# Staging the split output weights in the recurrent branch instead of the gating branch

## The chip, the cores and the metric

The kernel runs on one core of a Trainium2 chip. TensorE (PE) does the matmuls, VectorE (DVE), ScalarE (ACT) and GpSimd (POOL) the elementwise work, SyncE (SP) issues most loads. The time is that of one execution on the device in microseconds (us); less is better.

## What is computed

Two layers (DEPTH = 2) over 1024 tokens of width 1024. Each layer norms x, projects it through one input matrix `w_in`, runs three branches (a recurrent one, latent attention, and causal spatial gating, "SGU"), norms and gates the branches, and projects them through `w_out`:

```python
def spatial_gating(u, v, norm_g, norm_b, w_s, b_s):
    u = jax.nn.gelu(u)
    v = layer_norm(jax.nn.gelu(v), norm_g, norm_b)
    ...
# each layer:
#   x <- x + RMSNorm_post( W_out( concat_g RMSNorm_g( branch_g * SiLU(gate_g) ) ) )
# recurrent branch: h[t] = a[t] * h[t-1] + b[t], with a, b from gates of a short convolution of x
```

## The kernel before

All is float32, and every matmul is done in three passes over operands split in a high part and a remainder, hi x hi, hi x lo and lo x hi (`mm3`, L124 to L126). So each weight block must be split before it is used: ACT copies the high part, and POOL or DVE subtracts it to get the low part. For weights of `w_in` this is class `W` (loads at L366, ACT copy L375, subtract L376, on DVE for the columns `C_U` and `C_GC`, on POOL otherwise), for all else `split` (ACT copy L356, subtract L357).

A layer goes through these stages: the normed x is turned to feature rows hT; the recurrent branch runs in `group(g, half)`, six feature blocks in two halves of the tokens (convolution `conv`, gates `gate_in`, and for each of three blocks a chain of `lru_steps` that ends in a scan, L493, and L498); its steps wait in a list `pend` and are handed out a few at a time by `drain`. Then the SGU branch: a loop over eight token tiles with 512 columns (`toks` with the weights `C_U`, gelus L676 and L679, statistics L677 and L678), the turn of `sgu_w` (L691), the rope tables in layer 0 (among them L265, and L307), a loop over eight tiles with 256 columns (tanh L706 on ACT, then L707 on DVE, weights `wgc`), `sgu_mix` (L663) and a loop with the 352 columns of the latents (`C_LAT`). Attention and the output projection follow.

Large buffers come from a pool `FS` of seven slots F0 to F6 (rows of the result tile Y are lent to it), a first-in first-out list: a load into a slot waits until the last reader of the slot's former content is done. The register names R and H are smaller pools. A scheduler orders the instructions of each engine by a simulated timeline, so an engine's order is not the text's; each engine then runs its own order strictly.

Eight blocks of 128 rows of `w_out` (`wo0` to `wo7`) are split early in each layer and kept in DRAM, high parts `wo_h` and low parts `wo_l`, from where they are read in attention. `stage_wo(n)`, called once in each of the 16 steps of the two SGU loops, does it: in an even step it takes two slots and loads a block (SP, 512 KB, L615), in the odd step behind it ACT scales the block if it is one of the last three (L619) and copies the high part (L356), POOL subtracts (L357), ACT's queue stores the high part (L621), POOL's queue the low part (L622), and both slots are given back.

Of the kernel before, what the change touches and what calls it, by code (L numbers as in the profile page):

```python
# [8 lines left out]
F32R = mybir.dt.float32r  # L9
BF16 = mybir.dt.bfloat16  # L10
I32 = mybir.dt.int32
AF = mybir.ActivationFunctionType
# [75 lines left out]
def trunk_kernel(tc, A, out):  # L88
    nc = tc.nc
# [416 lines left out]
    def drain(n=1):  # L506
        for _ in range(n):
            if pend:
                pend.pop(0)()
# [39 lines left out]

    for l in range(DEPTH):  # L550

        xc, last, gw = {}, [], []

        def group(g, half):
            pss = [bank("PF") for m in range(2)]
# [5 lines left out]
            for m in range(2):  # L561
                f = 2 * g + m
                ps = pss[m]
                if g:
                    feat(ps, hT, ws[g], m, half)
                if f < 3:
                    if half == 0:
                        xc[f] = FS.take((128, 1024))
                    conv(l, f, half, ps, xc[f])
                    if half == 1:  # L570
                        steps = lru_steps(l, f, xc[f], gw)
                        pend.extend(steps[:-1])
                        last.append(steps[-1])
                else:
                    gate_in(ps, YA + f - 3, half)
                drain(3)
                if l == 0 and (g, half, m) == (0, 1, 0):
                    softplus_consts()
            if half == 1:
# [25 lines left out]
        pend.extend(last)  # L605
        pend.append(lambda: [RS.give(t) for t in gw])

        staged = {}

        def stage_wo(n):  # L610

            k, r = n // 2, W_ROWS[n // 2]
            if n % 2 == 0:
                staged[k] = FS.take((128, 1024)), FS.take((128, 1024))
                nc.sync.dma_start(out=staged[k][0], in_=A["w_out"][l, r:r + 128, :])  # L615
                return
            st, hi = staged.pop(k)
            if k >= 5:
                S_.activation(st, st, AF.Copy, scale=bgain(r // 128))  # L619
            split(st, hi.bitcast(F32R), st.bitcast(F32R), G)  # L620
            S_.dma_start(out=wo_dram[k][0], in_=hi)  # L621
            G.dma_start(out=wo_dram[k][1], in_=st)  # L622
            FS.give(st)
            FS.give(hi)


        for r in yrow[3:5]:
            FS.retire(r)
        vg, ug, gg = [], [], []

        def bgain(j):
            return par[:, 48 + l * 8 + j:49 + l * 8 + j]

        sg = HS.take((128, 2, 256))
        nc.sync.dma_start(out=sg[:, 0], in_=A["sgu_norm_g"][l].partition_broadcast(128))
# [34 lines left out]
        for t in range(NT):  # L670
# [9 lines left out]
            if t == 3:  # L680
                pend.extend([lambda: sgu_norm(0), lambda: sgu_affine(0)])
            drain(2)
            stage_wo(t)
        w.give()
        drain(100)
        sw = HS.take((128, 4, 128))
# [14 lines left out]
        for t in range(NT):  # L701
# [6 lines left out]
                                   op0=ALU.add, op1=ALU.mult)  # L708
            HS.give(th)
            drain(2)  # L710
            stage_wo(8 + t)
        w.give()
        drain(100)
        HS.give(sg)
# [432 lines left out]
```

## Time and profile before

| | us |
|---|---|
| median of 3 runs (lowest, highest) | 927.14 (925.89, 928.77) |
| profiled execution: its time | 928.23 |
| profiled execution: its span | 926.5 |
| PE busy in it | 879.8 |
| DVE busy | 568.7 |
| ACT busy | 520.1 |
| POOL busy | 425.4 |

The span runs from the first to the last instruction; the 1.7 us beside it lie around the program. Times of rows are counted from the span's start. PE is the busiest engine; what it doesn't do in the span are its waits.

### The profile page before, as it was taken

What the parts mean: (1) busy time and instruction counts of PE and PEld (TensorE: products, weight loads), DVE (VectorE), ACT (ScalarE), POOL (GpSimd) and SP (SyncE); (2) the same over time, 40 slices, a digit from 0 to 9 for tenths busy, and PEclk for the clock granted to TensorE, in tenths of its full rate; (3) what the DMA queues carried; (4) which work ended last, traced back from release to release, by engine and by line L of the source; (5) the groups of instructions that cost most, each with busy time, mean ns of one, the idle gap of its engine ahead of it and who ended that gap; (6) DMA issues with size and microseconds to landing.
All of it is one profiled execution on the core that took longest, in us unless ns stands there. A gap on an engine that the chain in (4) does not pass through costs nothing. (4 is left out here: it accounts for less than half of the span.)

```text
span 926.5 us, 13666 instructions
## 1 busy us (share of the span) xinstructions
PE 879.8 (95%) x5078; PEld 778.1 (84%) x5078; DVE 568.7 (61%) x1078; ACT 520.1 (56%) x1032; POOL 425.4 (46%) x461
## 2 busy tenths in 40 slices
PE   4999997999999999989999999989989999999996
PEld 3998786998889889868887888889978999998786
DVE  4567955735689897454456488434554989853322
ACT  6447744554777778444544386354466877754312
POOL 4720056564045567384743000665530567655822
PEclk9999998999999999998999999999999999999999
DMA  7201365322000253022324022753110015221322
GB/s 274 55 25 49 110 226 178 123 100 59 14 1 4 89 182 115 23 91 87 118 93 122 1 80 86 288 201 131 49 23 0 1 47 193 81 69 46 126 102 91
DMA packets 45080, 86.93 MB, mean 94 GB/s; under 512 B 8825, under 2 KB 26837, under 8 KB 45013
## 3 DMA queue, kind: packets, MB, share of 16 engines
q1 hardware_dynamic: 35796, 52.50, 17.8%
q0 software_dynamic: 6912, 25.17, 7.7%
q10 hardware_dynamic: 2304, 8.39, 2.3%
q8 instruction: 40, 0.66, 0.3%
q14 instruction: 28, 0.22, 0.1%
HBM read 60.88 MB, written 25.17 MB: 93 GB/s over the span
## 5 line engine op out<-in xcount | busy, mean ns | idle before, releaser
L124 PE MATMUL pw<-R,R 128*128 128x512 f32 (+1 forms) x704 | 259.7, 370 | 5.1 <-DVE R L357 2.1
L126 PE MATMUL pw<-R,R 128*128 128x512 f32 (+1 forms) x704 | 253.0, 360 | 0.7 <-POOL R L376 0.7
L125 PE MATMUL pw<-R,R 128*128 128x512 f32 (+1 forms) x704 | 253.3, 360 | 0.0
L124 PE MATMUL pa<-R,R 128*128 128x512 f32 (+3 forms) x540 | 187.3, 349 | 11.6 <-DVE F L707 6.6
L125 PE MATMUL pa<-R,R 128*128 128x512 f32 (+3 forms) x540 | 186.1, 345 | 0.0
L126 PE MATMUL pa<-R,R 128*128 128x512 f32 (+3 forms) x540 | 185.2, 345 | 0.0
L124 PEld LDWEIGHTS pw<-R,R 128*128 128x128 f32 x704 | 135.0, 192 | 25.7 <-ACT F L937 2.7
L126 PEld LDWEIGHTS pw<-R,R 128*128 128x128 f32 x704 | 134.9, 192 | 19.1 <-POOL R L376 1.1
L125 PEld LDWEIGHTS pw<-R,R 128*128 128x128 f32 x704 | 135.2, 192 | 17.2
L124 PEld LDWEIGHTS pa<-R,R 128*128 128x128 f32 x540 | 102.0, 189 | 22.5 <-DVE F L707 7.1
L939 POOL TENSOR_SCALAR F<-F,ring 128x128 f32<-128x128 f32 (+3 forms) x96 | 72.7, 762 | 89.5 <-DVE ring L938 87.9
L126 PEld LDWEIGHTS pa<-R,R 128*128 128x128 f32 x540 | 101.8, 189 | 9.9
L125 PEld LDWEIGHTS pa<-R,R 128*128 128x128 f32 x540 | 102.2, 189 | 8.6
L357 DVE TENSOR_TENSOR R<-pa,R 128x512 fp32r<-128x512 f32 (+1 forms) x120 | 73.9, 630 | 16.7 <-ACT R L356 15.7
L937 ACT ACTIVATE F<-pw,ring 128x128 f32<-128x128 f32 (+3 forms) x96 | 71.1, 743 | 21.1 <-DVE ring L935 18.4
L935 DVE TENSOR_REDUCE ring<-pw 128x1 f32<-128x128 f32 (+3 forms) x96 | 71.6, 749 | 11.3 <-PE pw L928 10.7
L356 ACT ACTIVATE R<-pa 128x512 fp32r<-128x512 f32 (+1 forms) x120 | 63.8, 554 | 19.2 <-PE pa L959 17.6
L376 POOL TENSOR_TENSOR R<-F,R 128x1024 fp32r<-128x1024 f32 (+1 forms) x24 | 54.2, 2265 | 42.2 <-ACT R L375 42.2
L968 PE MATMUL pa<-R,R 128*128 128x256 f32 x480 | 72.1, 288 | 0.5 <-DVE R L357 0.5
L968 PEld LDWEIGHTS pa<-R,R 128*128 128x128 f32 x480 | 63.4, 189 | 3.6 <-DVE R L357 1.1
L959 PE MATMUL pa<-ident,F 128*128 128x128 f32 x432 | 63.6, 273 | 0.7 <-DVE H L892 0.4
L357 POOL TENSOR_TENSOR R<-Y,R 128x640 fp32r<-128x640 f32 (+2 forms) x34 | 48.9, 1455 | 27.4 <-ACT R L356 10.2
(300 smaller groups left out, 1360.8 us busy)
## 6 DMA issues: line engine op xcount, KB each, us to landing
F<-in_w_in SPq DMA_DIRECT2D x24, 512.0 KB, 4.7
F<-in_x SPq DMA_DIRECT2D x13, 512.0 KB, 4.7
F<-in_w_out SPq DMA_DIRECT2D x9, 512.0 KB, 3.5
F<-x SPq DMA_DIRECT2D x8, 512.0 KB, 4.5
Y<-in_w_out SPq DMA_DIRECT2D x7, 512.0 KB, 4.4
x<-F SPq DMA_DIRECT2D x7, 512.0 KB
out_y<-F SPq DMA_DIRECT2D x7, 512.0 KB
Y<-in_w_in SPq DMA_DIRECT2D x6, 512.0 KB, 3.6
```

What stands on the lines that cost most here:

```text
L124: PE.matmul(ps, lhsT=sh, rhs=mh, start=start, stop=False)
L125: PE.matmul(ps, lhsT=sh, rhs=ml, start=False, stop=False)
L126: PE.matmul(ps, lhsT=sl, rhs=mh, start=False, stop=stop)
L356: S_.activation(h, src, AF.Copy)
L357: (eng or G).tensor_tensor(out=lo, in0=src, in1=h.bitcast(F32), op=ALU.subtract)
L376: self.eng.tensor_tensor(out=lo, in0=st, in1=h.bitcast(F32), op=ALU.subtract)
L935: V.tensor_reduce(out=mx, in_=sv, axis=AX.XY, op=ALU.max, negate=True)
L937: S_.activation(p[:, 0:n].rearrange("p (a b) -> p a b", a=sv.shape[1]), sv, AF.Exp, bias=mx, accum_out=sm)
L939: G.tensor_scalar(out=p[:, 0:n], in0=p[:, 0:n], scalar1=rs, scalar2=1.0, op0=ALU.mult, op1=ALU.mult)
L959: PE.transpose(pv[:, c, i * 128:(i + 1) * 128], p[i][:, b * 128:(b + 1) * 128], ident)
L968: PE.matmul(o, lhsT=sv, rhs=pt[:, part, c * 256:(c + 1) * 256], start=(b == 0 and part == 0), stop=(b == nb - 1 and part == 1))
```

## The change

`stage_wo` moves into the recurrent branch. It is called in `group`, behind `drain(3)`, in nine of the steps with `n` from 0 to 8, and each call does two things: it splits and stores the block that the call before loaded, and loads the next. So a block is loaded one step ahead of its split. Only the slot of the load is taken at the load; the slot of the high part is taken at the split. The operations, their number, their bytes and their engines are the same. The two calls in the SGU loops are gone.

```diff
--- before.py
+++ after.py
@@ -549,7 +549,26 @@
 
     for l in range(DEPTH):
 
-        xc, last, gw = {}, [], []
+        xc, last, gw, staged = {}, [], [], []
+
+        def bgain(j):
+            return par[:, 48 + l * 8 + j:49 + l * 8 + j]
+
+        def stage_wo(n):
+
+            if staged:
+                k, st = n - 1, staged.pop()
+                hi = FS.take((128, 1024))
+                if k >= 5:
+                    S_.activation(st, st, AF.Copy, scale=bgain(W_ROWS[k] // 128))
+                split(st, hi.bitcast(F32R), st.bitcast(F32R), G)
+                S_.dma_start(out=wo_dram[k][0], in_=hi)
+                G.dma_start(out=wo_dram[k][1], in_=st)
+                FS.give(st)
+                FS.give(hi)
+            if n < 8:
+                staged.append(FS.take((128, 1024)))
+                nc.sync.dma_start(out=staged[0], in_=A["w_out"][l, W_ROWS[n]:W_ROWS[n] + 128, :])
 
         def group(g, half):
             pss = [bank("PF") for m in range(2)]
@@ -574,6 +593,9 @@
                 else:
                     gate_in(ps, YA + f - 3, half)
                 drain(3)
+                n = 4 * half + 2 * g + m - 1 if g < 2 else 7 + 2 * half + m
+                if 0 <= n <= 8:
+                    stage_wo(n)
                 if l == 0 and (g, half, m) == (0, 1, 0):
                     softplus_consts()
             if half == 1:
@@ -605,31 +627,10 @@
         pend.extend(last)
         pend.append(lambda: [RS.give(t) for t in gw])
 
-        staged = {}
-
-        def stage_wo(n):
-
-            k, r = n // 2, W_ROWS[n // 2]
-            if n % 2 == 0:
-                staged[k] = FS.take((128, 1024)), FS.take((128, 1024))
-                nc.sync.dma_start(out=staged[k][0], in_=A["w_out"][l, r:r + 128, :])
-                return
-            st, hi = staged.pop(k)
-            if k >= 5:
-                S_.activation(st, st, AF.Copy, scale=bgain(r // 128))
-            split(st, hi.bitcast(F32R), st.bitcast(F32R), G)
-            S_.dma_start(out=wo_dram[k][0], in_=hi)
-            G.dma_start(out=wo_dram[k][1], in_=st)
-            FS.give(st)
-            FS.give(hi)
-
 
         for r in yrow[3:5]:
             FS.retire(r)
         vg, ug, gg = [], [], []
-
-        def bgain(j):
-            return par[:, 48 + l * 8 + j:49 + l * 8 + j]
 
         sg = HS.take((128, 2, 256))
         nc.sync.dma_start(out=sg[:, 0], in_=A["sgu_norm_g"][l].partition_broadcast(128))
@@ -680,7 +681,6 @@
             if t == 3:
                 pend.extend([lambda: sgu_norm(0), lambda: sgu_affine(0)])
             drain(2)
-            stage_wo(t)
         w.give()
         drain(100)
         sw = HS.take((128, 4, 128))
@@ -708,7 +708,6 @@
                                    op0=ALU.add, op1=ALU.mult)
             HS.give(th)
             drain(2)
-            stage_wo(8 + t)
         w.give()
         drain(100)
         HS.give(sg)
```

In the changed kernel the load is L571, the scale L563, the stores L565 and L566, the gelus L677 and L680; L356, L357, L366, L375 and L376 keep their numbers.

What stands on the engines in layer 0 now, at two places: where the recurrent branch hands over to the first token loop (ACT, SP, PE), and late in the SGU loops (ACT). First ACT at the hand-over, where the weights C_U for the first token loop are split. L375 splits C_U, L469, L470 and L481 are steps of the recurrence, L462 and L411 its gates, L676 the first gelu. Before:

```order
L375 ACTIVATE R1_102<-F5_139 128x1024
L462 ACTIVATE F6_140<-pa1_66,hb_85 128x512
L411 ACTIVATE H0_141<-pa2_67 128x512
L375 ACTIVATE R30_131<-F1_135 128x1024
L462 ACTIVATE Y_82<-pa0_65,hb_85 128x512
L481 ACT_TABLE_LOAD
L481 ACTIVATE Y_82<-Y_82 128x1024
L462 ACT_TABLE_LOAD
L462 ACTIVATE F3_137<-pa1_66,hb_85 128x512
L411 ACTIVATE H1_142<-pa3_68 128x512
L462 ACTIVATE Y_82<-pa0_65,hb_85 128x512
L375 ACTIVATE R15_116<-F1_135 128x1024
```

After:

```order
L356 ACTIVATE F6_140<-F3_137 128x1024
L462 ACTIVATE F5_139<-pa1_66,hb_85 128x512
L563 ACTIVATE F4_138<-F4_138,par_84 128x1024
L565 DMA wo5h_155<-F6_140 128x1024
L481 ACT_TABLE_LOAD
L481 ACTIVATE Y_82<-Y_82 128x1024
L356 ACTIVATE Y_82<-F4_138 128x1024
L411 ACT_TABLE_LOAD
L411 ACTIVATE H1_142<-pa3_68 128x512
L565 DMA wo6h_157<-Y_82 128x1024
L375 ACTIVATE R30_131<-F6_140 128x1024
L356 ACTIVATE Y_82<-Y_82 128x1024
```

The copies (L356) of wo5, wo6 and wo7, the scale (L563) of wo6 and the stores of the high parts of wo5 and wo6 stand there now; the split of the fourth quarter of C_U, `R30<-F6`, has moved behind them, and F6 is the slot that wo5's high part had.

SP's order at the same place, from the loads of the second halves of W2 on; L571 loads w_out, L366 with 2x512 loads a quarter of C_U, with 4x256 half of `wgc`. Before:

```order
L366 DMA F3_137<-in_w_in 128x2x512
L366 DMA Y_82<-in_w_in 128x2x512
L366 DMA F5_139<-in_w_in 128x2x512
L635 DMA H2_143<-in_sgu_norm_g 128x256
L636 DMA H2_143<-in_sgu_norm_b 128x256
L366 DMA F1_135<-in_w_in 128x2x512
L687 DMA H0_141<-in_sgu_w 128x4x128
L366 DMA F1_135<-in_w_in 128x4x256
L366 DMA Y_82<-in_w_in 128x4x256
```

After:

```order
L571 DMA F3_137<-in_w_out 128x1024
L366 DMA Y_82<-in_w_in 128x2x512 x2
L571 DMA Y_82<-in_w_out 128x1024
L636 DMA H2_143<-in_sgu_norm_g 128x256
L637 DMA H2_143<-in_sgu_norm_b 128x256
L571 DMA F4_138<-in_w_out 128x1024
L687 DMA H0_141<-in_sgu_w 128x4x128
L366 DMA F2_136<-in_w_in 128x2x352
L366 DMA F6_140<-in_w_in 128x2x512
L366 DMA F3_137<-in_w_in 128x2x512
L366 DMA F0_134<-in_w_in 128x4x256
L366 DMA Y_82<-in_w_in 128x4x256
```

Loads of w_out stand ahead of and between the quarters of C_U; the fourth and the third come, in this order, behind the load of wo6 (F4) and go to F6 and F3, slots of wo5, and a quarter of the latent weights (2x352) stands ahead of them.

PE at the first token matmuls; R31, R0, R1, R2 are the first two quarters of C_U, R3 and R32 high and low part of the third, pw0 to pa3 are banks, one for each token tile, and pa0 and pa1 with R24 and R25 are gates of the recurrence. Before:

```order
L124 MATMUL pw0_63<-R1_102,R6_107 128x512
L125 MATMUL pw0_63<-R2_103,R6_107 128x512
L126 MATMUL pw0_63<-R1_102,R7_108 128x512
L124 MATMUL pw0_63<-R3_104,R8_109 128x512
L125 MATMUL pw0_63<-R32_133,R8_109 128x512
L126 MATMUL pw0_63<-R3_104,R9_110 128x512
L124 MATMUL pw0_63<-R3_104,R8_109 128x512
L125 MATMUL pw0_63<-R32_133,R8_109 128x512
```

After:

```order
L124 MATMUL pa3_68<-R1_102,R18_119 128x512
L125 MATMUL pa3_68<-R2_103,R18_119 128x512
L126 MATMUL pa3_68<-R1_102,R19_120 128x512
L124 MATMUL pa1_66<-R13_114,R24_125 128x512
L125 MATMUL pa1_66<-R14_115,R24_125 128x512
L126 MATMUL pa1_66<-R13_114,R25_126 128x512
L124 MATMUL pw0_63<-R3_104,R8_109 128x512
L124 MATMUL pw1_64<-R3_104,R8_109 128x512
L124 MATMUL pa2_67<-R3_104,R20_121 128x512
L124 MATMUL pa3_68<-R3_104,R20_121 128x512
L125 MATMUL pw0_63<-R32_133,R8_109 128x512
L126 MATMUL pw0_63<-R3_104,R9_110 128x512
```

Before, the first tile goes on from the second quarter to the third at once. Now the first two quarters of four tiles (48 matmuls) come first, and R3 and R32 are read behind them.

Last, ACT in the second half of the SGU loops; L676 and L679 (before) and L677 and L680 (after) are gelus, L375 splits latent weights. Before:

```order
L356 ACTIVATE R27_128<-Y_82 128x1024
L619 ACTIVATE F1_135<-F1_135,par_84 128x1024
L676 ACTIVATE Y_82<-pa2_67 128x256
L679 ACTIVATE F4_138<-pa2_67 128x256
L375 ACTIVATE R31_132<-F6_140 128x704
L375 ACTIVATE R1_102<-F3_137 128x704
L356 ACTIVATE F6_140<-F1_135 128x1024
L375 ACTIVATE R3_104<-F5_139 128x704
L621 DMA wo5h_155<-F6_140 128x1024
L676 ACTIVATE Y_82<-pa3_68 128x256
L679 ACTIVATE F4_138<-pa3_68 128x256
```

After:

```order
L677 ACTIVATE F1_135<-pa2_67 128x256
L680 ACTIVATE F3_137<-pa2_67 128x256
L677 ACTIVATE Y_82<-pw0_63 128x256
L680 ACTIVATE Y_82<-pw0_63 128x256
L375 ACTIVATE R31_132<-F2_136 128x704
L375 ACTIVATE R1_102<-F5_139 128x704
L677 ACTIVATE Y_82<-pw1_64 128x256
L680 ACTIVATE Y_82<-pw1_64 128x256
L375 ACTIVATE R3_104<-F6_140 128x704
L677 ACTIVATE F1_135<-pa3_68 128x256
L680 ACTIVATE F3_137<-pa3_68 128x256
```

The scale L619, the copy L356 `F6<-F1` and the store of wo5 are gone from between the gelus; the splits of the latent weights remain.

## Rows read from the trace of the kernel before

**Rows 1.** Busy times of the page: us, share of the span, instructions.
```profile
PE 879.8 (95%) x5078; PEld 778.1 (84%) x5078; DVE 568.7 (61%) x1078; ACT 520.1 (56%) x1032; POOL 425.4 (46%) x461
```

**Rows 2.** PE's waits: engine, line, waited for: total us, times, longest us.
```profile
PE pa L124 <- DVE F L707: 6.6, 2, 6.4
...
PE pw L124 <- DVE R L357: 2.1, 1, 2.1
PE pa L124 <- ACT F L780: 1.6, 1, 1.6
PE pa L124 <- DVE R L347: 1.6, 1, 1.6
...
PE pw L306 <- DVE MQ L307: 1.2, 1, 1.2
...
PE pw L124 <- ACT F L679: 0.8, 1, 0.8
...
PE pw L126 <- POOL R L376: 0.7, 1, 0.7
```

**Rows 3.** Busy us by stretch: PE, PEld, DVE, ACT, POOL, clock, DMA share.
```profile
80.00:100.00 20.00, 20.00 (x90) 16.56 (x89) 17.14 (x18) 15.23 (x18) 0.00 (x0) 1.00 0.32 93
```

**Rows 4.** ACT's, then DVE's timeline: start, duration, [idle before <- releaser].
```profile
151.81 1.06 ACT L356 ACTIVATE F<-F 128x1024 fp32r<-128x1024 f32 x1 [1.25 <-POOL R L376]
...
153.46 0.36 ACT L676 ACTIVATE Y<-pa 128x256 f32<-128x256 f32 x1
...
153.85 0.43 DVE L677 BATCH_NORM_STATS2 bst<-Y 128x6 f32<-128x256 f32 x1 [4.25 <-ACT Y L676]
...
158.20 0.41 DVE L707 SCALAR_TENSOR_TENSOR F<-H,pa 128x256 f32<-128x256 f32 x1
```

**Rows 5.** The columns of rows 3 for a stretch of 2 us.
```profile
156.00:158.00 2.00, 0.00 (x0) 0.00 (x0) 1.93 (x3) 0.00 (x0) 1.85 (x3) 0.50 0.00 0
```

**Rows 6.** PE's timeline: first token matmul, around the wait, layer 1's first.
```profile
99.28 0.39 PE L124 MATMUL pw<-R,R 128*128 128x512 f32 x1
...
158.67 0.58 PE L124 MATMUL pa<-R,R 128*128 128x256 f32 x1 [6.40 <-DVE F L707]
...
162.85 0.28 PE L124 MATMUL pw<-R,R 128*128 128x256 f32 x1
...
558.82 0.39 PE L124 MATMUL pw<-R,R 128*128 128x512 f32 x1
```

**Rows 7.** POOL's w_out splits in slots F: busy us, mean ns | idle before.
```profile
L357 POOL TENSOR_TENSOR F<-F,F 128x1024 fp32r<-128x1024 f32 x8 | 19.2, 2407 | 71.7 <-ACT F L356 71.6
```

**Rows 8.** DVE's timeline: the first scan of both layers.
```profile
90.61 2.28 DVE L493 TENSOR_TENSOR_SCAN F<-Y,F 128x1024 f32<-128x1024 f32 x1
...
546.05 2.29 DVE L493 TENSOR_TENSOR_SCAN Y<-Y 128x1024 f32<-128x1024 f32 x1
```

**Rows 9.** DMA issues: count, KB each, median us to landing.
```profile
F<-in_w_in SPq DMA_DIRECT2D x24, 512.0 KB, 4.7
...
F<-in_w_out SPq DMA_DIRECT2D x9, 512.0 KB, 3.5
...
wo1l<-Y POOLq DMA_DIRECT2D x1, 512.0 KB, 8.3
wo3h<-F ACTq DMA_DIRECT2D x1, 512.0 KB, 2.6
...
wo6h<-Y ACTq DMA_DIRECT2D x1, 512.0 KB, 4.1
```

**Rows 10.** Timeline: POOL's split, DVE's L650 under it and later alone.
```profile
143.05 2.39 POOL L357 TENSOR_TENSOR F<-F,F 128x1024 fp32r<-128x1024 f32 x1 [3.84 <-ACT F L356]
...
144.13 2.39 DVE L650 TENSOR_TENSOR Y<-Y,H 128x1024 f32<-128x1024 f32 x1
...
165.11 1.21 DVE L650 TENSOR_TENSOR Y<-Y,H 128x1024 f32<-128x1024 f32 x1
```

**Rows 11.** One piece of the chain that ended last, layer 1.
```profile
677.93 2.94 DMA F<-in_w_uq
```

## Prediction

> **What bounds the kernel now.** I read the busy times first: TensorE (PE) is busy 879.8 of 926.5 us, so at most 46.7 us of the span can be won without shortening a matmul [rows 1]. So the question is which of PE's waits the change touches. The list of PE's waits answers that [rows 2]: one of 6.4 us for L707, VectorE's (DVE) step of the gate loop, is the longest single one, the waits for L357 (2.1), L780 (1.6) and L307 (1.2) lie in that branch or right behind it, and the one for L679 (0.8) lies where the recurrent branch hands over to the tokens. In the recurrent branch itself PE has no gap: 20.00 of 20 us, 90 matmuls, in 80:100 [rows 3]. For the 6.4 us I followed the chain on ScalarE (ACT) and DVE [rows 4]. ACT waits 1.25 us for a slot that POOL frees, copies a w_out block into it at 151.81, splits latent weights, and only at 153.46 comes to the last token's gelu L676; PE stood since 152. DVE sits idle 4.25 us for this gelu, then does steps of the rope table and reaches L707 at 158.20; PE's next matmul is at 158.67 [rows 6]. So in this stage the w_out work in ACT's queue ends the longest wait, and DVE's rope steps add to it. A second loss comes behind it: in 156:158 the granted clock is 0.50, the lower of the two levels (1.2 of 2.4 GHz) [rows 5], after PE had done nothing for the time of that wait, and from 158.67 to 162.85 PE does 19 matmuls of 256 columns in 4.18 us, 0.22 each [rows 6]. At the full clock they would take about half: 1.9 us lost.
>
> **What is moved, and what it costs.** Each of the 8 blocks of a layer takes a copy of 1.06 us on ACT [rows 4], three also a scale of the same size (I take the same time), and POOL 2.41 us [rows 7], beside two stores. 11 x 1.06 = 11.7 us of ACT and 8 x 2.41 = 19.3 us of POOL per layer leave the two SGU loops and enter the recurrent branch. The counts don't change, so nothing is won in work; all depends on what covers it. There ACT has room (15.23 of 20 us busy) and POOL is empty (0.00), but DVE is at 17.14 [rows 3].
>
> *Layer 0, SGU branch.* After the change ACT's queue has only gelus and latent splits here. The 6.4 us wait, its clock loss of 1.9 and the wait of 1.2 for L307 behind it (the rope steps no longer run late) go: 9.5. DVE's rope steps stay, so I keep 1.0 (0 to 2) back: -8.5.
>
> *Layer 0, hand-over.* The wait of 0.8 us goes, as PE now has four half tiles to do ahead: -0.8. A new one comes, and this is the term on which the sign rests. The copy of wo5 writes to the slot that the scan L493 of feature 0 frees, and the load of wo6 goes to another slot that it frees. The scan ends now at 90.61 + 2.28 = 92.89 [rows 8]. Five extra ACT operations (5.3 us) and the POOL splits of wo3 and wo4 come ahead of it; I take 2.4 us later (0 to 4.8, two splits), so 95.3. Then the wo6 load (3.5 us [rows 9]) lands at 98.8, its scale on ACT ends at 99.9, and only behind that scale, in ACT's order, stands the store of wo5's high part. It takes 2.6 to 4.1 us [rows 9]: 102.5 to 104.0. Only then may the fourth quarter of the weights C_U load into that slot (3.5 to 4.7 us, from the w_out row and the w_in row): 106.0 to 108.7. ACT's split (as a copy, 1.06) and DVE's (a step of 1024 columns, 1.21 [rows 10]) follow, and on DVE behind these the scan of feature 1 (2.28), L498 and the split of the third quarter (1.21 each), which PE reads first: 113.0 to 115.7. PE's first token matmul of now is at 99.28 [rows 6]; in the new order 48 matmuls of half tiles, 6 of an LRU gate and 4 that use the high part alone come ahead, 58 x 0.222 = 12.9 (20 us / 90, rows 3): it needs the low part at 112.2. So the stall is 0.8 to 3.5; I take 2.0. The store of wo5's low part on POOL's queue gives the slot for the third quarter: 95.3 + 1.06 + 2.41, then 2.6 to 8.3 us [rows 9] and a load: 104.9 to 111.8, later than the first path only at its slow end.
>
> *DVE held by POOL.* The trace shows a price that lies in no duration of one instruction. L650 on DVE takes 1.21 us when POOL is idle, and 2.39 at 144.13, where POOL's split of a w_out block ran from 143.05 to 145.44: it ends 1.08 us after POOL does [rows 10]. So a DVE operation that reads two SBUF operands and begins under a POOL subtract stands still until that ends. The Trainium skill says the same on the page SBUF — State Buffer, section Who interferes with whom: a DVE instruction with two SBUF inputs and a GpSimd instruction that reads SBUF exclude each other, and whoever issues first holds the shared port for its whole instruction. By that rule, the trace agrees, each moved split can cost DVE up to its own length, while a sum by durations alone would leave this term at nothing. Nearly all of DVE's work between the first scan and the last C_U split is of this kind, and the splits of wo5, wo6 and wo7 fall there: at most 3 x 2.41 = 7.2 us, less what DVE would wait for the fourth quarter anyway (its own work from 95.3, eight operations of about 1.21, ends at 105.0, and the quarter is split on ACT at 107.1 to 109.8). So 0 to 5.1; I take 2.0, in the lower half since POOL may also wait where DVE began first. Hand-over of layer 0 in all: +4.0 (0.8 to 8.6).
>
> The Trainium skill's page DMA: Bandwidth & Descriptors, section Anatomy of one DMA, gives 2.0 us plus bytes / 436e3 for a transfer on the GpSimd path, an estimate of 3.2 us for 512 KB. By it the store of wo5's low part would land at 102.0 and never matter; the rows go up to 8.3 us, and they decide.
>
> *Layer 0, start.* The split of wo0 enters POOL ahead of two W splits, and its copy ACT ahead of the last turns of hT: from nothing, where they have slack, to 1.06, the copy; +0.5.
>
> *Layer 1.* Its SGU waits of 2.1 and 1.6, and the 0.2 left of L707's 6.6, go; I keep 0.4 back: -3.5 [rows 2]. At the start the waits of 0.7 and 1.6 (L376, L347) go with the changed order of the groups, but the weights of the second group load behind two w_out loads and the x stores: at best 0.7 as now, at worst 3.0, most of another load; I take 1.7, so -0.6. Hand-over: the same chain, but the scan ends at 546.05 + 2.29 = 548.34 and the tokens begin at 558.82, 10.5 us, against 6.4 in layer 0: 4.1 more room [rows 6, 8]. So 0 to 4.5; I take 1.0. Late in the layer the w_uq weights load into other slots; their load has 2.94 us on the chain that ended last [rows 11]. It may go, or stand there twice: -2.9 to +2.9; I take +0.5, as one of the two slots is freed later.
>
> **Sum.** Layer 0: -8.5 - 0.8 + 4.0 + 0.5 = -4.8. Layer 1: -3.5 - 0.6 + 1.0 + 0.5 = -2.6. In all -7.4 on the profiled execution's 928.23 us, which stands 1.1 above the median of 927.14: 920.8 for an execution like the profiled one, 919.7 as a median; I say **920**.
>
> **Rivals.**
> 1. *Hand-over fully hidden.* If the stores land at the quick end and DVE isn't held, the 5.0 us of new stalls vanish: 919.7 - 5.0, about 915 (912 to 916). For it: DVE has 2 to 5 us to spare there. Against it: L650.
> 2. *The SGU stall is not only w_out's.* DVE takes 4.3 us from the gelu to L707 [rows 4]. If these steps still lie ahead, half of the 6.4 stays, with half of the drop of the clock: +3.2 and 1.0, so about 924 (922 to 926).
> 3. *Gain and price cancel.* With hand-overs of 8 to 11 us together 923 to 926 by the sum, with a worse start or w_uq 925 to 930.
> 4. *Slower: POOL's splits hold DVE through the recurrent branch.* 19.3 us of POOL per layer enter a stretch where DVE has under 3 us free in 20 [rows 3]. If 13 of them land on the chain of the scans in layer 0 (a stall of 13 + 1.9 for the clock, in place of 4.0) and 6 in layer 1 (in place of 1.0), the time is 919.7 + 10.9 + 5.0 = 935.6 (930 to 938). It decides once the two hand-overs together exceed 5.0 + 7.4 = 12.4 us, the clock's loss included. For it: the splits stand on the chain that frees the very slots into which C_U loads, so delays add. Against it: wo0 to wo4 are split before the first scan's operations begin.
>
> That the change doesn't do what it says is excluded: in the new order no w_out row is left in the SGU stretch.
>
> **Chances.** Forecast (917 to 923) 0.42, rival 1 0.18, rival 2 0.12, rival 3 0.11, rival 4 0.17. About 0.3% (2.8 us) is what a measurement of this kernel can tell from no change: 924.4 to 929.9 is the same. Faster: 0.42 + 0.18 + half of rival 2 = 0.66; same: the other half and most of rival 3, 0.15; slower: 0.19. The range 913 to 931 leaves out rival 4's larger part and the edge of rival 1; the forecast's own range is 917 to 923.
>
> **What the new profile would show.** The PE wait for L707 near 155 us gone, and the clock 1.00 there; POOL's idle time before w_out splits (71.7 us [rows 7]) much smaller; a new PE wait for DVE's L376 or ACT's L375 between 110 and 117 us, and a smaller one or none near 560; SP waiting for the stores of wo4 and wo5 ahead of C_U's loads; DVE operations of 2 to 3.5 us where 1.21 was. I am wrong if the wait in the SGU branch is still there under another name, or if the hand-over of either layer stands still for over 8 us.

## The result and the profile after

| | before | after |
|---|---|---|
| median of 6 runs each, us (lowest, highest) | 927.16 (925.89, 929.88) | 932.66 (930.60, 935.39) |
| ratio, 95% interval | | 1.0056 (1.0037 to 1.0076) |
| profiled execution: time, span | 928.23, 926.5 | 931.9, 930.1 |

The change makes the kernel 5.5 us slower. The forecast was 7 us faster, so the sign is wrong, and the time lies 1.7 us above the range. Ratios are not those of the medians, but worked out over the single executions, so they differ from them a little. Of all executions in this document three took over 1,200 us (one each of the kernel before and of l1_only and late_hi, two kernels of the experiments); the medians count them, which moves none by more than 0.4 us, and the ratios leave them out.

The busy times of the changed kernel's page, against [rows 1]. DVE has the same 1078 instructions and is busy 18.2 us longer; POOL and ACT are as before.

```profile
PE 884.8 (95%) x5078; PEld 779.3 (84%) x5078; DVE 586.9 (63%) x1078; ACT 521.2 (56%) x1033; POOL 425.5 (46%) x461
```

PE's waits after, against [rows 2]. The wait of 6.4 us in the SGU branch is gone, and so are those of layer 1 for L357 (2.1) and L780 (1.6). New ones are the waits for the gates of the recurrence (L462) and for the split of C_U (L376). In attention the waits for L936 (L937 before) grow from 1.0 to 3.9 us in all, the longest from 0.4 to 2.9.

```profile
PE pa L124 <- ACT F L462: 5.5, 4, 2.0
...
PE pw L125 <- DVE R L376: 4.1, 2, 3.7
PE pw L124 <- ACT F L936: 3.9, 4, 2.9
PE pw L124 <- DVE Y L707: 1.8, 1, 1.8
...
PE pa L124 <- DVE Y L707: 0.6, 1, 0.6
```

The same columns as [rows 3], for stretches of the changed kernel; the last row is the kernel before. In 80:100 PE was full and is now busy 17.15 us at 0.91 of the clock; the SGU stretch 140:160, in which the old wait stood, is full at 1.00; at 120 us the clock is at 0.50, its lower level; in 800:820, far behind the change, PE is busy 17.10 us at 0.91, against 19.69 at 1.00 before.

```profile
80.00:100.00 20.00, 17.15 (x68) 13.35 (x66) 14.80 (x21) 15.18 (x18) 0.00 (x0) 0.91 0.10 31
96.00:98.00 2.00, 2.00 (x6) 1.57 (x5) 1.97 (x3) 2.00 (x3) 0.00 (x0) 0.50 0.14 45
...
120.00:122.00 2.00, 0.65 (x2) 0.56 (x3) 1.29 (x2) 0.67 (x2) 0.00 (x0) 0.50 0.88 233
120.00:140.00 20.00, 18.65 (x72) 15.26 (x73) 12.17 (x15) 13.98 (x15) 2.30 (x1) 0.84 0.30 89
140.00:160.00 20.00, 20.00 (x105) 17.15 (x104) 11.05 (x20) 7.53 (x19) 6.33 (x5) 1.00 0.07 19
...
800.00:820.00 20.00, 17.10 (x111) 15.82 (x111) 17.84 (x30) 13.43 (x31) 14.88 (x22) 0.91 0.34 106
...
800.00:820.00 20.00, 19.69 (x140) 18.43 (x139) 16.30 (x35) 16.30 (x38) 17.01 (x24) 1.00 0.34 108
```

Since PE's order changes, stages are compared by PE's lag: the start of a certain PE instruction, less the columns of all matmuls ahead of it at 0.222 us per 512 columns (the rate of [rows 3]). What the lag grows by in a stage is what PE loses there; only differences between kernels mean something. The stages end at the turn of the parameters (start), the first turn of `sgu_w` in layer 0 (recurrent branch and first token loop), the first turn L340 for layer 1 (SGU branch to the end of layer 0), the last L340 (begin of layer 1), the turn of `sgu_w` in layer 1, and the end of the span. All kernels of this study, each from its profiled execution, in us:

```
            start  recurrent L0  SGU.. L0  begin L1  recurrent L1  rest   span
before       20.5       6.5        48.4      8.4        7.1        48.3   926.5
after        18.3      19.6        41.4      7.5        9.7        46.4   930.1
l0_only      20.7      17.4        41.7      7.0        6.9        49.3   930.3
l1_only      18.6       6.6        47.4      7.1       10.6        46.5   924.0
late_hi      20.7       6.6        45.5      9.0        5.9        48.3   923.1
no_scale     20.5      16.8        44.2      7.7       12.2        41.2   929.8
no_sub       18.4      16.1        42.3      8.4       12.2        46.5   931.1
neither      20.4      12.2        42.6      8.6       12.9        46.3   930.2
neither2     18.8       7.5        41.4      9.1       12.3        47.7   924.0
sub_v        18.7      15.9        42.8      9.4        8.3        49.9   932.2
late7        20.4      16.9        42.3      8.1        9.6        49.1   933.5
five         19.7      12.2        38.3      8.0       10.1        48.8   924.3
after_y16    18.3      17.4        41.7      9.4       10.9        42.5   927.4
five_y16     20.4       9.5        39.8      8.4       11.1        44.5   920.8
```

The start is either 18.3 to 18.8 or 19.7 to 20.7, and kernels of the same layer 0 stand in both groups (before and l1_only), so it is not the change. One program's stage also varies by about 2 us: layer 0 is the same in after, l0_only and after_y16, and its recurrent branch is at 19.6, 17.4 and 17.4. The change costs 10.9 to 13.1 us there and gives back 6.7 to 7.0 in the SGU branch. A profiled execution can also lie up to 3 us off the median of its kernel: l1_only's (925.81) and late_hi's (924.91) are the fastest of their twelve, sub_v's (933.96) is 2.9 under its median. So a row of the table shows where PE loses time, and the medians show how much.

How the hand-over comes to be late, engine by engine. PE's timeline first: three waits for gates of the recurrence, then one for the split of the third quarter of C_U.

```profile
84.18 0.51 PE L124 MATMUL pa<-R,R 128*128 128x512 f32 x1 [0.89 <-ACT F L462]
...
94.86 0.50 PE L124 MATMUL pa<-R,R 128*128 128x512 f32 x1 [1.96 <-ACT F L462]
...
115.48 0.50 PE L124 MATMUL pa<-R,R 128*128 128x512 f32 x1 [1.03 <-ACT F L462]
...
121.35 0.79 PE L125 MATMUL pw<-R,R 128*128 128x512 f32 x1 [3.73 <-DVE R L376]
```

ACT's timeline, and as its last row the load of wo7 in SP's. At 82.41 stands the scale of wo7. Its load waits in SP for a slot and is issued only at 77.80, 0.7 us after ACT is free for the scale; ACT waits 5.32 us in all, 4.6 of them from that issue on. The gates L462 and the first step of the scan's chain, L469, stand behind it. At 112.20 ACT waits again, for the C_U quarter that loads into wo5's slot.

```profile
76.40 0.69 ACT L462 ACTIVATE F<-pa,hb 128x512 f32<-128x512 f32 x1
82.41 1.15 ACT L563 ACTIVATE Y<-Y,par 128x1024 f32<-128x1024 f32 x1 [5.32 <-DMA Y<-in_w_out]
83.46 0.67 ACT L462 ACTIVATE F<-pa,hb 128x512 f32<-128x512 f32 x1
...
85.55 1.24 ACT L469 ACTIVATE Y<-F,k 128x1024 f32<-128x1024 f32 x1
...
112.20 1.06 ACT L375 ACTIVATE R<-F 128x1024 fp32r<-128x1024 f32 x1 [2.48 <-DMA F<-in_w_in]
...
77.80 0.34 SPq L571 DMA_DIRECT2D Y<-in_w_out  x1
```

DVE's timeline, and behind it POOL's splits. The four splits shown each find a DVE operation beside them: a conv step of three columns takes 2.18 us (0.20 at 65.37, alone), a step of the constants of six columns, L224, 2.37, the step L474 2.88 and the second scan 4.46 (the first, alone, 2.29 against 2.28 in [rows 8]). The splits of wo2 (55.64) and wo6 (107.90) cost DVE nothing and 0.2 us. The first scan begins at 97.18 against 90.61.

```profile
61.03 2.18 DVE L443 SCALAR_TENSOR_TENSOR Y<-tails,par,Y 128x3 f32<-128x3 f32 x1
...
65.37 0.20 DVE L443 SCALAR_TENSOR_TENSOR Y<-tails,par,Y 128x3 f32<-128x3 f32 x1
...
67.64 2.37 DVE L224 TENSOR_SCALAR ring<-par 128x6 f32<-128x6 f32 x1
...
80.92 0.17 DVE L252 TENSOR_SCALAR k<-k 128x6 f32<-128x6 f32 x1
...
97.18 2.29 DVE L493 TENSOR_TENSOR_SCAN F<-F,F 128x1024 f32<-128x1024 f32 x1
...
101.11 2.88 DVE L474 TENSOR_SCALAR Y<-Y 128x1024 f32<-128x1024 f32 x1
...
114.44 4.46 DVE L493 TENSOR_TENSOR_SCAN F<-Y,F 128x1024 f32<-128x1024 f32 x1
...
120.08 1.22 DVE L376 TENSOR_TENSOR R<-F,R 128x1024 fp32r<-128x1024 f32 x1
...
60.80 2.39 POOL L357 TENSOR_TENSOR F<-F,F 128x1024 fp32r<-128x1024 f32 x1 [1.90 <-ACT F L356]
...
67.50 2.48 POOL L357 TENSOR_TENSOR Y<-Y 128x1024 fp32r<-128x1024 f32 x1 [3.44 <-ACT Y L356]
...
100.66 2.78 POOL L357 TENSOR_TENSOR F<-F,F 128x1024 fp32r<-128x1024 f32 x1 [29.81 <-ACT F L356]
...
114.30 2.45 POOL L357 TENSOR_TENSOR Y<-Y 128x1024 fp32r<-128x1024 f32 x1 [2.72 <-ACT Y L356]
```

Last, attention in layer 1, where nothing was changed: DVE's product L979 (0.42 us in the kernel before) stands 3.86 us beside two operations L938 and a split on POOL, and PE waits 2.90 us for what follows. The first row is DVE's, then POOL's, then PE's; the last two are DVE's and POOL's in the kernel before.

```profile
806.05 3.86 DVE L979 TENSOR_TENSOR Y<-Y,H 64x256 f32<-64x256 f32 x1
...
806.30 2.10 POOL L938 TENSOR_SCALAR F<-F,ring 128x896 f32<-128x896 f32 x2
808.37 1.25 POOL L357 TENSOR_TENSOR R<-H,R 128x512 fp32r<-128x512 f32 x1
...
811.13 0.51 PE L124 MATMUL pw<-R,R 128*128 128x512 f32 x1 [2.90 <-ACT F L936]
...
806.57 0.42 DVE L980 TENSOR_TENSOR Y<-Y,H 64x256 f32<-64x256 f32 x1
...
807.13 2.12 POOL L939 TENSOR_SCALAR F<-F,ring 128x896 f32<-128x896 f32 x2
```

### The profile page after: what moved, and what is told of

Read it like the earlier page. It is cut to its first block, busy times and chain, and to the rows that moved or that the text cites. A ratio compares the mean times of both kernels' runs of the same rounds, so it can differ in the third digit from the quotient of the medians.

```text
span 930.1 us, 13661 instructions
## 1 busy us (share of the span) xinstructions
PE 884.8 (95%) x5078; PEld 779.3 (84%) x5078; DVE 586.9 (63%) x1078; ACT 521.2 (56%) x1033; POOL 425.5 (46%) x461
## 3 DMA queue, kind: packets, MB, share of 16 engines
q1 hardware_dynamic: 35796, 52.50, 18.3%
## 4 chain that ended last, share of the span: by engine, by line
PE 49%; DVE 4%; DMA 2%; ACT 2%; POOL 2%; issue 1%; DVEq 0%; POOLq 0%; SPq 0%; ACTq 0%
PE pw L124 9%; PE pw L125 9%; PE pw L126 9%; PE pa L124 4%; PE pa L126 4%; PE pa L125 4%; PE pa L967 4%; PE pa L958 3%; DMA F<-in_w_in 1%; POOL R L357 1%; ACT F L936 1%; DMA wo5h<-F 1%; PE pw L927 1%; PE pa L340 1%; POOL R L376 1%
## 5 line engine op out<-in xcount | busy, mean ns | idle before, releaser
L126 PEld LDWEIGHTS pa<-R,R 128*128 128x128 f32 x540 | 102.3, 190 | 10.1
L938 POOL TENSOR_SCALAR F<-F,ring 128x128 f32<-128x128 f32 (+3 forms) x96 | 72.7, 761 | 63.3 <-DVE ring L937 62.3
L936 ACT ACTIVATE F<-pw,ring 128x128 f32<-128x128 f32 (+3 forms) x96 | 71.1, 741 | 28.2 <-DVE ring L934 22.9
L357 DVE TENSOR_TENSOR R<-pa,R 128x512 fp32r<-128x512 f32 (+1 forms) x120 | 73.9, 629 | 17.1 <-ACT R L356 15.9
L967 PE MATMUL pa<-R,R 128*128 128x256 f32 x480 | 74.4, 291 | 0.3 <-DVE R L357 0.2
L356 ACT ACTIVATE R<-pa 128x512 fp32r<-128x512 f32 (+1 forms) x120 | 63.5, 553 | 18.8 <-PE pa L958 16.6
L376 POOL TENSOR_TENSOR R<-F,R 128x1024 fp32r<-128x1024 f32 (+1 forms) x20 | 44.8, 2256 | 45.7 <-ACT R L375 45.7
L1095 POOL TENSOR_TENSOR F<-F,F 128x1024 f32<-128x1024 f32 (+2 forms) x20 | 39.3, 1964 | 47.6 <-DVE F L1002 47.4
```

The lines of the kernel that those rows point to most:

```text
L126: PE.matmul(ps, lhsT=sl, rhs=mh, start=False, stop=stop)
L356: S_.activation(h, src, AF.Copy)
L357: (eng or G).tensor_tensor(out=lo, in0=src, in1=h.bitcast(F32), op=ALU.subtract)
L376: self.eng.tensor_tensor(out=lo, in0=st, in1=h.bitcast(F32), op=ALU.subtract)
L936: S_.activation(p[:, 0:n].rearrange("p (a b) -> p a b", a=sv.shape[1]), sv, AF.Exp, bias=mx, accum_out=sm)
L938: G.tensor_scalar(out=p[:, 0:n], in0=p[:, 0:n], scalar1=rs, scalar2=1.0, op0=ALU.mult, op1=ALU.mult)
```

## The experiments

Times are medians; ratios are against the kernel before in runs beside them: its median was 926.11 beside l0_only, l1_only, no_scale and no_sub, 926.81 beside late_hi, neither, sub_v and five, and 927.51 beside the other four.

**One layer at a time.** `l0_only` and `l1_only` keep the old `stage_wo`, as `stage_old`, in the two SGU loops of the other layer. The edit of l0_only, cut; in l1_only the layer is 1:

```diff
-                if 0 <= n <= 8:
+                if l == 0 and 0 <= n <= 8:
...
             drain(2)
+            if not (l == 0):
+                stage_old(t)
...
             drain(2)
+            if not (l == 0):
+                stage_old(8 + t)
```

> Layer 0 staged in the recurrent branch, layer 1 in the SGU loops as before. By the traces the changed layer 0 is 5.1 us behind at the first rotation of attention (207.26 against 202.19). Theory 1 (the loss is made at the hand-over of layer 0, where ACT waits for a load of w_out ahead of the recurrence): about +4 to +5, 931 to 932 us, with the PE waits for L462 and L376 between 84 and 122 us and the low clock behind them as in the changed kernel. Theory 2 (the moved POOL splits cost the same in either layer): half of the 5.5, about 930.

> Layer 1 staged in the recurrent branch, layer 0 in the SGU loops as before. Theory 1: layer 1 by itself gains: the SGU waits (3.9) and the wait for w_uq (about 5) go, the hand-over costs 2.4, so 921 to 925 us, less if the 2.9 us wait in attention near 811 us and the clock behind it (4.5 together) come again. Theory 2 (POOL's splits cost the same in either layer): about 930.

Measured: l0_only 931.87, 1.0059 (1.0038 to 1.0080); l1_only 927.89, 1.0024 (1.0004 to 1.0043). The loss lies for the most part in layer 0, 5.8 us by the medians: its recurrent branch takes 10.9 us more and the SGU branch 6.7 less. Layer 1 alone is 1.8 us slower by the medians, so the 921 to 925 of theory 1 didn't come. The table shows +3.5 in its recurrent branch and less ahead of it and behind it, +1.3 in all; and l1_only has the meeting in attention too (2.90 us at 804.93), for which theory 1 allowed 4.5 us more. l0_only has it not.

**The slot of the high part in the old place.** `late_hi` is the kernel before, with the second slot taken at the split and not at the load.

```diff
-                staged[k] = FS.take((128, 1024)), FS.take((128, 1024))
+                staged[k] = FS.take((128, 1024))
...
-            st, hi = staged.pop(k)
+            st, hi = staged.pop(k), FS.take((128, 1024))
```

> The kernel before with one part of the change alone: staging stays in the SGU loops, but the slot of the high part is taken at the split and not at the load. If the SGU wait came from slots held too long, ACT's copies come earlier and the 6.4 us wait shrinks: 922 to 925 us. If it came from the copies' place in ACT's queue and DVE's rope steps, 925 to 928.

Measured: 927.14, 1.0008 (0.9993 to 1.0023). The wait for L707 falls from 6.4 to 3.5 us in the profile, the stage by 2.9, and the median does not move; the execution profiled is the fastest of its twelve. So slots held early are part of that wait, and a later take alone is worth nothing that can be measured.

**The suspects of the hand-over, one at a time.** `no_scale` does without the scale, `no_sub` without POOL's subtraction.

```diff
-                if k >= 5:
-                    S_.activation(st, st, AF.Copy, scale=bgain(W_ROWS[k] // 128))
```

> The changed kernel with the scale of the last three blocks (L563) left out: those rows of w_out go unscaled. Theory 1 (ACT stands 5.3 us at the scale of wo7, waiting for its load, with the recurrence of feature 0 queued behind it): the scan of feature 0 ends 5 to 7 us earlier, the PE waits of 0.9 and 2.0 for L462 and the low clock of 95 to 99 us go, 5 us, and the later stall of 3.7 shrinks: 924 to 927 us. Theory 2 (what counts is POOL's hold of DVE): only six operations of 1.15 us less on ACT, 930 to 932.

```diff
-                split(st, hi.bitcast(F32R), st.bitcast(F32R), G)
+                S_.activation(hi.bitcast(F32R), st, AF.Copy)
```

> The changed kernel with POOL's subtraction of the w_out blocks left out: the whole block is stored in place of its low part. Theory 2 (POOL's subtract holds DVE operations with two SBUF operands, 2.2 us each): the DVE operations of 2.9 to 4.5 us at the hand-over (L474 and L493 in layer 0; L475, L480 and L493 in layer 1) are back at 0.7 to 2.3, the stalls of 3.7 and 2.4 us go, with the clock's 2.6: 924 to 926 us. Theory 1: the wait of ACT for wo7 and the PE waits near 84 and 95 us stay; if they are all that counts, 930 to 932.

Measured: no_scale 931.75, 1.0078 (1.0053 to 1.0104); no_sub 931.60, 1.0056 (1.0037 to 1.0076). Both times are in the range of the theory that the other suspect is all that counts. Neither alone gives back more than 3.5 us of the stage, or 1.3 against the 17.4 of l0_only and after_y16. In no_scale L469 no longer waits for a load, but for its constants, which DVE makes and which are late (DVE's conv steps are held as in the changed kernel); then three DVE operations are held (2.83, 2.78 and the scan's 4.36), and one long wait is left, beside one of 1.52. ACT's row, then PE's:

```profile
84.26 1.25 ACT L469 ACTIVATE Y<-F,k 128x1024 f32<-128x1024 f32 x1 [2.14 <-DVE k L252]
...
119.56 0.80 PE L124 MATMUL pa<-R,R 128*128 128x512 f32 x1 [7.02 <-ACT F L462]
```

In no_sub DVE's operations have their normal lengths (L474 0.67, the second scan 2.22) and DVE is busy 566.4 us, 20.5 less than after. The wait at the hand-over is 2.00. But with its subtractions gone the scheduler orders the start otherwise: PE waits 3.27 us in the convolution and, in layer 1, 3.54 for a split of W. PE's and DVE's rows:

```profile
43.23 0.47 PE L124 MATMUL pw<-R,R 128*128 128x512 f32 x1 [3.27 <-DVE Y L440]
...
113.59 0.73 PE L124 MATMUL pw<-R,R 128*128 128x512 f32 x2 [2.00 <-ACT R L375]
...
498.44 0.61 PE L124 MATMUL pw<-R,R 128*128 128x512 f32 x1 [3.54 <-ACT R L375]
...
102.25 0.67 DVE L474 TENSOR_SCALAR Y<-Y 128x1024 f32<-128x1024 f32 x1
```

**Both at once.** `neither` joins both edits; in `neither2` the first two blocks keep their subtraction, so that the order ahead of the convolution stays that of the changed kernel. Its diff:

```diff
-                if k >= 5:
-                    S_.activation(st, st, AF.Copy, scale=bgain(W_ROWS[k] // 128))
-                split(st, hi.bitcast(F32R), st.bitcast(F32R), G)
+                S_.activation(hi.bitcast(F32R), st, AF.Copy)
+                if k < 2:
+                    G.tensor_tensor(out=st.bitcast(F32R), in0=st, in1=hi, op=ALU.subtract)
```

> The changed kernel with both left out, the scale (L563) and POOL's subtraction of the w_out blocks. Taken out alone, neither helped: without the scale the recurrence of feature 0 still began at 84.26, as it then waited for the constants k from DVE, 6 us late by POOL's splits of wo3 and wo4 and a changed order; without the subtraction DVE's operations had their own length, but ACT still waited for the load of wo7. Theory 3 (two delays side by side, each covers the other): with both out the first scan ends at 93 to 96, the hand-over stands still for 0 to 3 us, 920 to 926 us. Theory 4 (the chain from wo5's store to C_U's load sets the hand-over whatever comes ahead): a stall of 4 to 7 us with the low clock behind it, 929 to 932.

> The changed kernel with the scale of blocks 5 to 7 left out and POOL's subtraction left out for blocks 2 to 7 (the stores write unsplit rows there); copies, loads, stores and their order stay. The first two subtractions stay, so that the order ahead of the convolution is the changed kernel's. Theory: ACT's wait behind the scale and DVE's stops under POOL's subtractions together make up the hand-over in layer 0; without both the stage loses 12 to 15 us in place of 24.1 (11.0 in the kernel before) and the time is 918 to 925. Rival: the chain of loads and stores alone sets the hand-over: stage 20 or more, time 928 to 932.

Measured: neither 931.30, 1.0045 (1.0028 to 1.0062), stage 12.2 of which 2.45 are again a wait in the convolution at 43.43; neither2 924.76, 0.9976 (0.9962 to 0.9991), stage 7.5. (The expectations of neither2 and late7 count the stage from another mark: their 24.1 and 11.0 are the table's 19.6 and 6.5.) The time of neither is one that theory 4 gave, but its stall of 4 to 7 us is not there: the wait at the hand-over is 1.41. With the start's order kept, the stage of neither2 is within 1.0 us of the kernel before's 6.5, though all loads, copies and stores stand in the recurrent branch: of the cost of 10.9 to 13.1 the two suspects carry 9.9 to 12.1 together. With the scale go its wait and three ACT operations of 1.15 us, with the subtraction the stops of DVE and POOL's 2.4 us ahead of each store of a low part; what is left of the chain of loads, copies and stores makes one wait of 0.61 us. One thing stays: the first scan begins at 94.77, still 4.2 us later than in the kernel before. The constants are late without any hold, as DVE's order is another one here and puts other work between their steps: L252, for which L469 waits, ends at 81.74, against 76.33 before and 81.09 after. So the later scan by itself costs PE little. PE's row, then DVE's:

```profile
105.32 0.73 PE L124 MATMUL pw<-R,R 128*128 128x512 f32 x2 [0.61 <-ACT R L375]
...
81.57 0.17 DVE L252 TENSOR_SCALAR k<-k 128x6 f32<-128x6 f32 x1
...
94.77 2.28 DVE L493 TENSOR_TENSOR_SCAN F<-F,F 128x1024 f32<-128x1024 f32 x1
...
109.23 2.22 DVE L493 TENSOR_TENSOR_SCAN F<-Y,F 128x1024 f32<-128x1024 f32 x1
```

**The subtraction on DVE.** `sub_v` does it there for wo5 to wo7.

```diff
-                split(st, hi.bitcast(F32R), st.bitcast(F32R), G)
+                split(st, hi.bitcast(F32R), st.bitcast(F32R), V if k >= 5 else G)
```

> The changed kernel with the low parts of wo5, wo6 and wo7 subtracted on DVE (about 1.22 us each) in place of POOL. Theory 2 (each of these splits holds a DVE operation for 2.2 us): DVE's chain between the first scan and C_U's last quarter gets up to 3 x 1.0 us shorter, so the stall of 3.7 us shrinks: 929 to 931 us. Rival: DVE itself is the bound there and now waits for the load of wo6 and wo7 in its own order: 933 to 937.

Measured: 936.89, 1.0111 (1.0087 to 1.0135). The scan isn't held (2.28 at 115.40) and the stage falls to 15.9, but ACT's wait is still there (4.76 us at 81.65), and in the table 5.4 us are lost behind that stage against the changed kernel, 2.7 of them in a wait for L707 in layer 1. The time is in the rival's range, and theory 2 missed.

**wo7's split later.** `late7` calls its scale, split and stores two half tiles later.

```diff
-                n = 4 * half + 2 * g + m - 1 if g < 2 else 7 + 2 * half + m
+                n = 4 * half + 2 * g + m - 1 if g < 2 else (7, -1, -1, 8)[2 * half + m]
```

> The changed kernel with scale, split and stores of the last block two half tiles later, its load where it was; nothing is left out. Theory: ACT's wait for this block's load (5.3 us at 82.41), which stands ahead of the gates of the first scan, is a large part of the hand-over's cost; the first scan begins at 92 to 95 in place of 97.2, the stage from the parameters to the SGU's weights loses 17 to 21 us in place of 24.1, and the time is 927 to 930. Rival: the scan's constants and the later store of this block keep the hand-over as late as it was: stage 23 to 26, time 931 to 934.

Measured: 935.96, 1.0097 (1.0078 to 1.0116). The edit did not do what it was for: the scheduler put the scale at the same place, and ACT still waits 4.94 us there. Only wo7's copy came later, from 113.17 to 116.52. So it decides nothing about the scale. Its time lies outside both ranges, and why it is 3 us slower than the changed kernel is left open.

```profile
82.52 1.15 ACT L563 ACTIVATE Y<-Y,par 128x1024 f32<-128x1024 f32 x1 [4.94 <-DMA Y<-in_w_out]
...
116.52 1.06 ACT L356 ACTIVATE F<-Y 128x1024 fp32r<-128x1024 f32 x1 [1.36 <-DMA wo6l<-F]
```

**Half the move.** `five` does wo0 to wo4 in the recurrent branch and wo5 to wo7, in the old manner, in the first SGU loop.

```diff
-            if n < 8:
+            if n < 5:
...
-                if 0 <= n <= 8:
+                if 0 <= n <= 5:
                     stage_wo(n)
...
+            if t < 6:
+                stage_old(10 + t)
```

> Only wo0 to wo4, which need no scale, are staged in the recurrent branch; wo5 to wo7 in the first six steps of the first SGU loop in the old way. Theory 3: no w_out work of ACT or POOL stands between the first scan and C_U's last quarters, so the hand-over is as before (0 to 2 us), and three blocks in place of eight in the SGU loops leave less than half of the 6.4 us wait: 920 to 925 us. Rival: the splits of wo3 and wo4 alone delay the constants and so the scan by 4 us, and the SGU wait stays, since its ACT queue still carries copies: 926 to 930.

Measured: 926.56, 1.0000 (0.9981 to 1.0018), in the rival's range and not in that of theory 3. The first scan begins at 92.89 (97.18 after), the SGU stage is the shortest of all, 10.1 us under the kernel before; the recurrent branch gives 5.7 of it back in a wait of 2.78 us for a gelu at 116.47 with a low clock behind it (five_y16, the same in layer 0, has the wait without the low clock and gives back 3.0), that of layer 1 another 3.0.

**The meeting in attention.** `after_y16` and `five_y16` do that one product of layer 1 on POOL.

```diff
-            (V if units.index((h, j)) in Y_ON_V else G).tensor_tensor(out=yv, in0=yv, in1=tmp[mine], op=ALU.mult)
+            (V if units.index((h, j)) in Y_ON_V and (l, h, j) != (1, 4, 0) else G).tensor_tensor(out=yv, in0=yv, in1=tmp[mine], op=ALU.mult)
```

> The changed kernel with one product of layer 1's attention (L979 of head 4, first block of queries) on POOL in place of DVE; nothing is left out. In the changed kernel this product stood on DVE for 3.86 us at 806.05 behind POOL's work, where it takes 0.42 elsewhere, and PE waited 2.9 us for it and ran at less than the full clock after it; the kernel before has no such wait. Theory: about 4 us of the changed kernel's loss is this one meeting, so the time is 927.5 to 929.5 and the wait of 2.9 us is gone. Rival: whatever DVE begins there next is held in its place, or the product is late on POOL: 931 to 934.

> The version with blocks 0 to 4 in the recurrent branch and 5 to 7 in the first SGU loop, with the same product of layer 1 on POOL; nothing is left out. Theory: the two losses are separate, so it gains some 4 us on 926.6: 921.5 to 924, faster than the kernel before. Rival: the meeting moves elsewhere: 925.5 to 928.

Measured: after_y16 930.09, 1.0033 (1.0014 to 1.0051); five_y16 922.65, 0.9949 (0.9930 to 0.9968), faster than both kernels by 4.9 us (927.51 in the same runs) and 10.0 us (932.66). The rest stage falls by 3.9 and 4.3 us, the medians by 2.6 and 3.9; that of after_y16 is 0.6 above the range that the theory gave, that of five_y16 within it. The kernel before with that product on POOL was not run; its trace has no wait over 0.4 us there. PE is as full as before in that stretch of after_y16, and the product takes its time on POOL:

```profile
800.00:820.00 20.00, 19.69 (x139) 18.13 (x138) 16.24 (x36) 17.11 (x40) 18.71 (x26) 1.00 0.35 106
...
809.72 0.72 POOL L979 TENSOR_TENSOR Y<-Y,H 64x256 f32<-64x256 f32 x1
```

## Why the prediction was wrong

The terms of its sum against the stages of before and after:

| term | predicted | measured | from |
|---|---|---|---|
| layer 0, SGU branch | -8.5 | -7.0 | stage |
| layer 0, recurrent branch and hand-over (-0.8, +4.0, start +0.5) | +3.7 | +13.1 (10.9 in l0_only) | stage |
| layer 1, start | -0.6 | -0.9 | stage |
| layer 1, hand-over | +1.0 | +2.6 | stage; waits 1.58, 0.41, 0.38 |
| layer 1, SGU branch | -3.5 | -3.7 | waits of 2.13 and 1.62 gone |
| layer 1, w_uq | +0.5 | -3.0 | waits of 1.33, 1.54, 0.52 gone, 0.42 left |
| meeting in attention | none | +4.5 | 2.90 and the clock of 0.91 (at most 1.8); -3.9 to -4.3 when taken away |
| sum | -7.4 | +5.5 (median) | terms +5.6, stages without the start +5.9 |

**What was right.** The SGU branch: the wait for L707 and the low clock behind it are gone in layer 0, both waits in layer 1. Its size was 1.5 us off: waits of 0.6 and 1.8 us for L707 remain at 171 and 175, where 1.0 was kept back. (Its loss of 1.9 to the low clock is 2.1 by its own rows: 19 matmuls in 4.18 us, which take 0.11 each at the full clock.)

**The step that failed is the hand-over of layer 0**, +4.0 in the sum and +10.9 to +13.1 in the stage. The wait for which the term was made came almost as sized, 3.73 us at C_U's split. That is luck: the split ended at 121.30, where 113.0 to 115.7 was worked out, and PE came to it at 117.6, where 112.2 was, so both were over 5 us late. PE was late because of what the sum had at nothing: three waits for the gates, 3.9 us, and the clock. It went wrong in three places.

*"Five extra ACT operations (5.3 us) ... I take 2.4 us later."* The first scan ended 6.6 us later (99.47 against 92.89), beyond the bound of 4.8. The operations were counted by their lengths. But a scale waits for a load, and the load for a slot: ACT stood 5.3 us at the scale of wo7, with the gates and L469 of the chain behind it. The copies of wo5 and wo6 were traced with their loads, and this scale, which the scheduler puts ahead of both, was not. The scale is not all of the scan's delay: without it (no_scale) the scan begins at 97.14, and 4.2 of the 6.6 us are still there in neither2.

*"DVE held by POOL ... I take 2.0."* The mechanism was right; the price was over twice the 2.0, though within the 0 to 5.1. L474 and the second scan lost 2.2 us each, on the chain, so 4.4 for two splits. The prediction also argued against more by saying that wo0 to wo4 are split before the first scan's operations begin. They are, but they too hold DVE, at a convolution step and at the making of the constants (2.0 and 2.2 us). L252 ended at 81.09 against 76.33, and in no_scale it is the constants that hold the scan. What these two holds cost PE is not shown, since the constants are as late in neither2, which has no such hold.

*The clock.* The hand-over had no term for it. Four waits make 7.6 us; behind them the clock was at the lower level twice, and 80:100 at 0.91 (1.8 us) and 120:140 at 0.84 (3.2 us) add up to 5.0, a part of which falls into the last wait itself (in 120:122 PE is busy 0.65 us). Together at most 12.6, against 13.1 by the stage. The clock's part is not the same in every execution: after_y16, with the same layer 0, had 1.00 in 80:100 and 0.91 in 120:140, and its stage is 2.2 us shorter.

That this is the cause is shown for the two suspects together (neither2), not for each one's share: taken alone, each leaves the other, with an order of its own, and neither2 too has an order of its own on DVE. Rival 4 came nearest. Its time (930 to 938) and its bound hold: the two stages grew by 13.1 + 2.6 = 15.7 us, over the 12.4 at which it said that the sign turns. Its mechanism holds in part: of the 13 us that it put on the chain of the scans, the trace shows 4.4, and ACT's wait for the load, which it did not have, is the other of the two.

**What was not foreseen** is the meeting in attention of layer 1, far behind the change. In the kernel before DVE's product begins 0.56 us ahead of POOL's operation (806.57 and 807.13) and takes 0.42; after, the two begin 0.25 us apart and it takes 3.86. Of the eleven other kernels of this study that keep the product on DVE, eight have a wait of 2.9 us there; l0_only, late_hi and no_scale have not. So it came with the move in layer 1, in all its kernels but no_scale, and never without it. No instruction of that part is changed, so I take it for a matter of when the two engines come there; only the product's part in it is shown, by after_y16. The w_uq loads went the other way by about as much, -3.0 where the prediction's bound was -2.9.

## What to carry to other kernels

When work moves onto an engine that runs in strict order, trace every load that its moved operations wait for, and what stands behind each of them; the length of an operation is the least that it costs. Before GpSimd elementwise work is moved beside a chain on VectorE, price each such operation at up to its full length on VectorE (here 2.2 us of 2.4), however small the VectorE operation that meets it, and look for the clock behind any new wait. A gain may still be had from a part of the move: five blocks in place of eight, with one product off the meeting, won 4.9 us.

## What the runs showed of the hardware that was not expected

Size protects nothing: a DVE operation on 3 columns took 2.18 us under POOL's split, and 0.20 alone, and one of 64 x 256 stood 3.86 us through three POOL operations in a row (2.10 for two, and 1.25), not through one. By the profile that one began 0.25 us ahead of POOL's first and was still the one that stood; times on POOL are rough, so which of the two was first is not settled. An operation with one SBUF input is held as well: L474 took 2.88 us under POOL's split and 0.67 in no_sub. The Trainium skill's page SBUF — State Buffer, section Who interferes with whom, has this too: `tensor_scalar` can run in modes that take both port pairs and then contends with GpSimd. The trace agrees, with 2.2 us for that one.
